# A two-layer attention trunk on one core: layer 0's SiLU gate in wide products, rope's swap in one operation, more gating from PSUM, and a new order

## The chip, the core and the metric

The kernel runs on one core of a Trainium2 chip. The metric is device microseconds for one execution, the median over runs. Five engines matter: TensorE (PE) multiplies, with its weight loads shown apart (PEld); VectorE (DVE) and ScalarE (ACT) do the elementwise work; GpSimd (POOL) does a few powers; the Sync engine (SP) issues the loads. Each engine takes its instructions in the order in which they are written and waits at semaphores.

## The reference

256 tokens of width 1024 pass two layers. Both normalise, project to queries, keys, values and a gate `z`, mix the tokens, multiply by `silu(z)`, project out and add; then each adds a projected embedding under a sigmoid gate.

```python
for i in range(DEPTH):                       # DEPTH = 2
    h = rms_norm(x, norm_gain[i])
    x = x + (moba_layer if i % 2 == 0 else nsa_layer)(h, ...)
    gate = jax.nn.sigmoid(rms_norm(x, ple_gate_gain[i]) @ ple_w_gate[i])
    x = x + gate * (p[i] @ ple_w_proj[i])

def moba_layer(h, w_in, q_gain, k_gain, w_out, pos):      # layer 0
    q, k, v, z = jnp.split(h @ w_in, 4, axis=-1)
    q = rope(rms_norm(split_heads(q, N_HEADS), q_gain), pos)
    k = rope(rms_norm(split_heads(k, N_HEADS), k_gain), pos)
    o = merge_heads(moba_attention(q, k, v)) * jax.nn.silu(z)
    return o @ w_out

def rope(x, pos):                                          # halves of a head change places
    x1, x2 = xf[..., :half], xf[..., half:]
    return jnp.concatenate([x1 * cos - x2 * sin, x2 * cos + x1 * sin], axis=-1)
```

With 256 tokens and blocks of 256, layer 0 is causal attention over 16 heads of 64. Layer 1 has 16 query heads in 4 groups, and three branches per head (compressed keys, selected blocks, window), each weighted by a sigmoid and summed.

## The kernel before

Precision: a weight matrix arrives in float32 and is split into a high part (`hi`, rounded, written by ACT) and a low part (`lo`, the remainder, written by DVE). Activations are split the same way into a tile `a` that holds high and low side by side, 256 columns each. A product is `hi`x`a`-high + `hi`x`a`-low + `lo`x`a`-high.

Two classes hold the projections with features on the partitions. `Unit` takes 512 output features; for each slice of 128 of the contraction and each block of 128 features, `mul` issues three products of 256 columns into one half of a PSUM bank. `Wide` takes 256 features; it multiplies `hi` by both halves of `a` in one product of 512 columns, a whole bank, and adds `lo` x high as a product of 256 into the bank's left half. What leaves a `Wide` bank has to be joined: right half plus left half. The list `WIDE` names the projections done so: before, the output projections and embedding gates of both layers (`o0 o1 g0 g1`, and with `n` those of layer 1); `z0 z1`, layer 0's gate, are `Unit`s.

`tail` is the part of a layer from `z` on. A gate that comes from a `Unit` leaves through `evac_z` (512 columns, two blocks: scale by the token's norm, tanh, one product), one from a `Wide` through `evac_wz`, which no step before the change uses. Attention output for two blocks (a group, 0 to 3) stands in one bank of tag `tr`. Step `E<g>` copies it to `oT` by ACT, and `x.<k>` multiplies a block by its gate and splits it into `a`; step `G<g>` (`gate_o`) multiplies the bank by the gate in one DVE operation, and `x.<k>` then only splits. Before, every group goes through `E`.

In layer 1 the compressed branch of a group is added in one of two ways: step `<g>B` makes its transposed weights `pcT` and `pcL` ahead, and the group's `V` step then adds its four products to its own bank; or step `<g>b`, later, multiplies into a bank of its own, and DVE adds that to `oT`. Before, group 3 has a `B` and groups 0, 1 and 2 have a `b`.

`rope` works on 8 heads and two blocks of 128 tokens. Per block, `turn` multiplies the swapped halves by the sine table: `turn(t, 0)` and `turn(t, 1)`, 256 columns each. Seven ropes run: four in layer 0 (`q`, `k`, `1q`, `1k`), three in layer 1 (`KE`, `QE0`, `QE1`).

The order: `PROGRAM` is a list of some 500 steps, written out by hand. A step records operations, and a planner (`Plan.schedule`) with a cost per operation then sets each engine's order among all that is ready, earlier-recorded first; it may also move an operation made with `nc.copy` from ACT to DVE. In the list, `w:name.i` loads and splits a weight tile, `name.i` multiplies it, `name>b` empties a bank; `A S T V` are a head pair's transposes, scores, transposed weights and products with the values. Buffers limit what can run ahead: five of each of `raw`, `hi`, `lo` and `tmp`, four PSUM banks `mm`, two `tr`, two `s`.

Of the kernel before, what the change touches and what calls it, by code (L numbers as in the profile page):

```python
# [19 lines left out]
SWITCH, POW = 150.0, 2300.0  # L20
NRAW, NHI, NLO, NPT, NA = 5, 5, 5, 9, 9
WARM = 14
WIDE, NARROW = "o0 o1 g0 g1 no0 no1 ng0 ng1", "ng1b"
MARGIN = 100.0

PROGRAM = ("x0 w:c0 c0 x1 w:c1 c1 x2 w:c2 x3 w:c3 x4 w:c4 w:k.0 x5 c2 w:c5 c3 x7 consts tq a.1 x6 a.3 a.5 a.6 w:c6 a.7 w:c7 "
# [24 lines left out]

STORES = 5

# [8 lines left out]
class View:  # L62
# [25 lines left out]
    def box(self):  # L88
        (ps, pn), free = self.ap.ap[0], self.ap.ap[1:]
        p0, f0 = divmod(self.ap.offset, ps)  # L90
        return p0, p0 + pn, f0, f0 + sum((n - 1) * s for s, n in free) + 1

    def elems(self):
        n = 1
# [326 lines left out]
def trunk(ctx: ExitStack, tc: tile.TileContext, a, out):  # L421
# [14 lines left out]
    def tmp(name):  # L436
        return work.tile([P, 512], F32, tag="tmp", name=name, bufs=5)
# [136 lines left out]
    class Wide:  # L574
# [2 lines left out]


        def __init__(self, src, xs, wide=True):
            self.src, self.xs, self.w, self.ps, self.wide = src, xs, {}, None, wide  # L580

        def weights(self, g):
            if self.ps is None:
# [85 lines left out]
    def rope(ps, tab, nb, norm, is_q, tag, bufs, o=None):  # L669
        if o is None:  # L670
            o = work.tile([P, 2, 512], F32, tag=tag, name=tag, bufs=bufs)
        else:
            ps = [o[:, t] for t in range(2)]
        o = o.rearrange("p t (h d) -> p t h d", d=HD)
        ssq = work.tile([P, 2, 8], F32, tag="ssq", name="ssq")
        for t in range(2):
            sq = tmp("hsq").rearrange("p (h d) -> p h d", d=HD)
            nc.scalar.activation(sq.rearrange("p h d -> p (h d)"), ps[t], AF.Square)
            nc.vector.tensor_reduce(ssq[:, t], sq, axis=AX.X, op=OP.add)
        r0 = work.tile([P, 2, 8], F32, tag="r0", name="r0")  # L680
        g = 8 // nb
        qss = [tmp("qs").rearrange("p (b g d) -> p b g d", b=nb, d=HD) for _ in range(2)]
        vs = [ps[t].rearrange("p (b g d) -> p b g d", b=nb, d=HD) for t in range(2)]

        def tb(i, t, lo, hi):
            return tab[:, i, t, :, None, lo:hi].to_broadcast([P, nb, g, hi - lo])

        def turn(t, c):
            lo, hi = 32 * c, 32 * c + 32
            nc.vector.tensor_tensor(qss[t][:, :, :, lo:hi], vs[t][:, :, :, 32 - lo:64 - lo], tb(1, t, lo, hi), op=OP.mult)  # L690

        since = len(nc.ops)
        for t in range(2):
            nc.vector.tensor_scalar(r0[:, t], ssq[:, t], 1.0 if is_q else 1.0 / HD,
                                    norm.e2[:, 0 if is_q else 1, t:t + 1], op0=OP.mult, op1=OP.add)

        turn(0, 0)
        nc.together(since)
        r = work.tile([P, 2, 8], F32, tag="r_" + tag, name="r_" + tag, bufs=bufs)
        nc.gpsimd.tensor_tensor(r.rearrange("p t h -> p (t h)"), r0.rearrange("p t h -> p (t h)"), neg_half, op=OP.pow)  # L700
        if is_q:
            nr = work.tile([P, 2, 8], F32, tag="nr_" + tag, name="nr_" + tag, bufs=bufs)
            nc.vector.tensor_scalar(nr, r, -1.0, None, op0=OP.mult)
        def finish():
            for t in range(2):
                ot = o[:, t].rearrange("p (b g) d -> p b g d", b=nb)
                if t:
                    turn(t, 0)
                turn(t, 1)
                nc.vector.tensor_tensor(ot, vs[t], tb(0, t, 0, HD), op=OP.mult)  # L710
                nc.vector.tensor_tensor(ot, ot, qss[t], op=OP.add)
                if not is_q:
                    nc.vector.tensor_tensor(o[:, t], o[:, t], r[:, t, :, None].to_broadcast([P, 8, HD]), op=OP.mult)

        return o, (nr if is_q else None), finish
# [13 lines left out]
    def flat(ap):  # L729
        return ap.rearrange("p a b -> p (a b)")  # L730
# [6 lines left out]
        nc.scalar.activation(th, zr, AF.Tanh, scale=0.5)  # L737
        nc.vector.scalar_tensor_tensor(flat(zz[:, m:m + 2]), flat(th), 1.0, flat(zr), op0=OP.add, op1=OP.mult)

    def evac_wz(zz, ps, m, norm):  # L740
        zr, th = tmp("zr")[:, :T], tmp("th")[:, :T]
        nc.scalar.activation(zr, ps[:, T:], AF.Copy)
        nc.vector.tensor_tensor(zr, zr, ps[:, :T], op=OP.add)
        nc.vector.tensor_tensor(zr, zr, norm.bc, op=OP.mult)
        nc.scalar.activation(th, zr, AF.Tanh, scale=0.5)
        nc.vector.scalar_tensor_tensor(zz[:, m], th, 1.0, zr, op0=OP.add, op1=OP.mult)

    def tail(i, oT, pvs, zin, xz, norm, after):

# [52 lines left out]
        def wide(kind, h, xs, evac):  # L802
            name = f"{n}{kind}{h}"
            if name not in WIDE.split():
                return False
            for q in range(2):
                u = Wide(a["w_" + name][q], xs, name + "ab"[q] not in NARROW.split()).steps(name + "ab"[q])
                for b in range(2):
                    todo[f"{name}{'ab'[q]}>{b}"] = lambda u=u, b=b, m=4 * h + 2 * q + b: evac(u, b, m)
            return True  # L810
# [23 lines left out]
                    after(k)  # L834

        for h in range(2):
            if not wide("z", h, xz, lambda u, b, m: evac_wz(zz, u.ps[b], m, norm)):
                u = Unit(zin[h], True, xz).steps(f"{n}z{h}")
                for b in range(2):
                    todo[f"{n}z{h}>{b}"] = lambda u=u, b=b, m=4 * h + 2 * b: evac_z(zz, u, b, m, norm)  # L840
# [698 lines left out]
```

## Time and profile before

| | |
|---|---|
| Median of 3 runs | 358.29 us (358.08 to 359.67) |
| Profiled execution | 359.04 us, span 357.2 us |
| Granted TensorE clock | 1.000 |
| Instructions in the span | 6734 |
| Read from memory | 57.46 MB, 164 GB/s over the span |
| Queues | 20160 of 20770 packets in SP's queue |

The profile's page gives busy time per engine, the chain of work that ended last, and groups of instructions (engine, operation, out<-in, shape, count, then busy us and the mean ns of one, then the idle time before them and what ended it). Nearly all operations carry the line of the planner's emitting loop (L399), so groups are told apart by tile names and shapes: `mm<-a,hi` is a projection's product, `tr<-cst,sm` a transpose of attention weights, `big` holds `oT`, gates and the like, `tq` and `tk` are rope's tables. Matmuls are pipelined, and the mean of one is longer than the distance from one to the next; distances are read from start times.

### The profile page before, as it was taken

Reading aid. Unit: us, or ns where it says so; the run is one execution under the profiler, and the core shown is the slowest. Engines: PE = TensorE matmul, PEld = TensorE weight load, DVE = VectorE, ACT = ScalarE, POOL = GpSimd, SP = SyncE. Lnnn points to the kernel's source line nnn. Section 1 sums busy time; section 2 is a strip of 40 time slices with the busy share of each in tenths; the row PEclk is TensorE's granted clock in tenths of the full one; section 3 lists DMA queues with packets and bytes.
Section 4 is the critical chain, followed back from the end, with each engine's and each line's share of the span. In section 5 each row is a group of like instructions: output and inputs, shape, how many; then the busy total and the mean of one; then the engine's idle time right before and its main releaser. Section 6 shows DMA issues by size and latency. Waiting matters only on the chain.

```text
span 357.2 us, 6734 instructions
## 1 busy us (share of the span) xinstructions
PE 351.3 (98%) x2327; PEld 308.4 (86%) x2327; DVE 334.0 (93%) x845; ACT 276.6 (77%) x614; POOL 30.0 (8%) x26
## 2 busy tenths in 40 slices
PE   8999999999999999999999999999999999999995
PEld 6788888888999888888889999866998989888884
DVE  4899999999999988989989999999999999999985
ACT  4775699998999865758844988968979999947632
POOL 1033200320000000010003300003000000000100
PEclk9999999999999999999999999999999999999999
DMA  7988665053653455664453625347573432166012
GB/s 249 338 332 274 232 218 194 1 184 132 200 166 117 153 176 171 190 198 153 127 175 100 237 75 178 120 150 284 205 240 137 125 111 63 61 217 194 0 47 73
DMA packets 20770, 58.95 MB, mean 165 GB/s; under 512 B 2560, under 2 KB 6016, under 8 KB 20736
## 3 DMA queue, kind: packets, MB, share of 16 engines
q1 hardware_dynamic: 20160, 58.04, 50.0%
q10 hardware_dynamic: 576, 0.48, 0.4%
q8 instruction: 18, 0.29, 0.3%
q14 instruction: 16, 0.13, 0.1%
HBM read 57.46 MB, written 1.05 MB: 164 GB/s over the span
## 4 chain that ended last, share of the span: by engine, by line
PE 97%; DMA 1%; DVE 0%; ACTq 0%; issue 0%; ACT 0%; DVEq 0%
PE mm L399 77%; PE tr L399 13%; PE s L399 6%; DMA tmp<-in_wq 1%; ACTq L399 0%; DVE tmp L399 0%; DVE hi L399 0%; ACT tmp L399 0%; DVE xT L399 0%; DVEq L1534 0%
## 5 line engine op out<-in xcount | busy, mean ns | idle before, releaser
L399 PE MATMUL mm<-a,hi 128*128 128x256 f32 (+1 forms) x656 | 154.0, 327 | 0.0
L399 ACT ACTIVATE hi<-raw 128x1024 fp32r<-128x1024 f32 (+2 forms) x100 | 99.6, 1007 | 35.3 <-PE mm L399 20.9
L399 DVE TENSOR_TENSOR lo<-raw,hi 128x1024 fp32r<-128x1024 f32 (+2 forms) x100 | 115.1, 1161 | 6.3 <-ACT hi L399 5.8
L399 PE MATMUL mm<-a,lo 128*128 128x256 f32 x448 | 104.6, 283 | 0.0
L399 PE MATMUL mm<-hi,a 128*128 128x512 f32 (+2 forms) x356 | 102.1, 377 | 0.5 <-DVE hi L399 0.5
L399 PEld LDWEIGHTS mm<-a,hi 128*128 128x128 f32 x656 | 101.2, 190 | 0.8 <-issue 0.2
L399 PEld LDWEIGHTS mm<-a,lo 128*128 128x128 f32 x448 | 83.2, 189 | 10.1
L399 PEld LDWEIGHTS mm<-hi,a 128*128 128x128 f32 x356 | 64.5, 191 | 11.9 <-ACT a L399 0.6
L399 PE MATMUL mm<-lo,a 128*128 128x512 f32 (+2 forms) x178 | 63.6, 374 | 0.0
L399 ACT ACTIVATE sm<-sm,nb 128x128 f32<-128x128 f32 (+1 forms) x96 | 42.6, 448 | 3.8 <-DVE nb L399 3.6
L399 PEld LDWEIGHTS mm<-lo,a 128*128 128x128 f32 x178 | 33.0, 188 | 5.4 <-DVE lo L399 0.2
L399 DVE CUSTOM_DVE_ANT_0 sm<-s,cst,nr_q 128x128 f32<-128x128 f32 (+1 forms) x96 | 35.8, 410 | 0.4
L399 ACT ACTIVATE tmp<-tmp 128x256 f32<-128x256 f32 (+3 forms) x26 | 12.2, 472 | 13.3 <-DVE tmp L399 13.0
L399 ACT ACTIVATE pt<-tr 128x384 f32<-128x384 f32 x48 | 21.7, 483 | 0.6 <-PE tr L399 0.3
L399 PE MATMUL tr<-cst,sm 128*128 128x128 f32 x144 | 22.0, 275 | 0.0
L399 POOL TENSOR_TENSOR r_q<-r,neg_half 128x16 f32<-128x16 f32 x5 | 14.6, 2925 | 76.9 <-DVE r L399 76.9
L399 PEld LDWEIGHTS tr<-cst,sm 128*128 128x128 f32 x144 | 16.8, 141 | 3.2 <-ACT sm L399 0.8
L399 POOL TENSOR_TENSOR rstd<-ms,neg_half 128x2 f32<-128x2 f32 x4 | 4.7, 1184 | 165.9 <-DVE ms L399 165.9
L399 ACT ACTIVATION_READ_ACCUMULATOR sm<-sm,nb 128x1 f32 x96 | 18.3, 191 | 0.0
L399 ACT ACTIVATE a<-xT,gain_in 128x256 fp32r<-128x256 f32 x31 | 14.5, 498 | 4.7 <-DMA xT<-in_x 1.9
L399 DVE TENSOR_TENSOR hl<-tr,hl 64x512 fp32r<-64x512 f32 x24 | 16.5, 689 | 1.7 <-ACT hl L399 1.1
L399 DVE TENSOR_SCALAR sm<-sm,l 128x128 f32<-128x128 f32 (+1 forms) x67 | 17.8, 315 | 0.1
(167 smaller groups left out, 453.1 us busy)
## 6 DMA issues: line engine op xcount, KB each, us to landing
raw<-in_moba_in SPq DMA_DIRECT2D x28, 512.0 KB, 4.5
raw<-in_nsa_in SPq DMA_DIRECT2D x24, 512.0 KB, 4.0
raw<-in_w_o SPq DMA_DIRECT2D x8, 512.0 KB, 3.9
raw<-in_w_g SPq DMA_DIRECT2D x8, 512.0 KB, 3.8
raw<-in_w SPq DMA_DIRECT2D x8, 512.0 KB, 3.7
raw<-in_w_no SPq DMA_DIRECT2D x8, 512.0 KB, 4.3
raw<-in_w_ng SPq DMA_DIRECT2D x8, 512.0 KB, 3.8
raw<-in_ple_proj SPq DMA_DIRECT2D x4, 512.0 KB, 4.1
```

Of the source, the lines that this page charges most:

```text
L399: getattr(getattr(self.nc, o.engine), o.method)(*[real(x) for x in o.args], **{k: real(x) for k, x in o.kwargs.items()})
```

## The change

Layer 0's gate is put on the list `WIDE`, so that its products are made by `Wide`, and `evac_wz` is rewritten to join two banks into one tile of 512 columns before it scales it. Rope's `turn` becomes one operation over both halves, with a reversed step over the axis of the halves (`View.box`, which finds what an operation touches, learns negative steps). The list uses `G2`, `G3` and `nG3` in the place of `E2`, `E3` and `nE3`, and `2B` in the place of `2b`. The list is written in another order from `masks` on; its last steps are as before.

```diff
-WIDE, NARROW = "o0 o1 g0 g1 no0 no1 ng0 ng1", "ng1b"
+WIDE, NARROW = "o0 o1 g0 g1 no0 no1 ng0 ng1 z0 z1", "ng1b"
...
-           "w:1q.0 w:1q.3 1q.0 masks w:1k.0 A2 S2 w:1k.2 w:1q.1 w:1q.2 A3 1k.0 1k.1 w:1v.0 S3 1q.1 1q.2 1q.3 1qe A0 1q T2 "
+           "w:1q.0 w:1q.3 1q.0 masks w:1k.0 v A3 S3 w:1q.1 1q.1 w:1q.2 1q.2 1q.3 w:1k.3 A2 w:1v.0 w:1v.1 A0 1qe S2 1q T3 "
...
-        def turn(t, c):
-            lo, hi = 32 * c, 32 * c + 32
-            nc.vector.tensor_tensor(qss[t][:, :, :, lo:hi], vs[t][:, :, :, 32 - lo:64 - lo], tb(1, t, lo, hi), op=OP.mult)
+        def turn(t):
+            v, q = (x.rearrange("p b g (c d) -> p (b g) c d", c=2) for x in (vs[t], qss[t]))
+            nc.vector.tensor_tensor(q, v[:, :, ::-1], tb(1, t, 0, HD).rearrange("p b g (c d) -> p b g c d", c=2), op=OP.mult)
...
-        turn(0, 0)
+        turn(0)
...
                 if t:
-                    turn(t, 0)
-                turn(t, 1)
+                    turn(t)
...
-    def evac_wz(zz, ps, m, norm):
-        zr, th = tmp("zr")[:, :T], tmp("th")[:, :T]
-        nc.scalar.activation(zr, ps[:, T:], AF.Copy)
-        nc.vector.tensor_tensor(zr, zr, ps[:, :T], op=OP.add)
-        nc.vector.tensor_tensor(zr, zr, norm.bc, op=OP.mult)
+    def join(u, m):
+        b, first = m % 2, u.sum is None
+        if first:
+            u.sum = tmp("sum")
+        half = u.sum[:, b * T:b * T + T]
+        nc.scalar.activation(half, u.ps[b][:, T:], AF.Copy)
+        nc.vector.tensor_tensor(half, half, u.ps[b][:, :T], op=OP.add)
+        return not first
+
+    def evac_wz(zz, u, m, norm):
+        if not join(u, m):
+            return
+        zr, th, m = u.sum, tmp("th"), m - m % 2
+        zr2 = zr.rearrange("p (a b) -> p a b", a=2)
+        nc.vector.tensor_tensor(zr2, zr2, norm.bc[:, None, :].to_broadcast([P, 2, T]), op=OP.mult)
         nc.scalar.activation(th, zr, AF.Tanh, scale=0.5)
-        nc.vector.scalar_tensor_tensor(zz[:, m], th, 1.0, zr, op0=OP.add, op1=OP.mult)
+        nc.vector.scalar_tensor_tensor(flat(zz[:, m:m + 2]), flat(th), 1.0, flat(zr), op0=OP.add, op1=OP.mult)
```

What this does to the engines' order is shown at three places. First TensorE, in layer 0's gate, before: `hi` and `lo` are the weight's parts (here the ones loaded, since features lie on the partitions), `a` the moving activations, `mm_78` and `mm_79` the two banks.

```order
L399 MATMUL mm_78<-a_112,hi_117 128x256 x2
L399 MATMUL mm_78<-a_112,lo_122 128x256
L399 MATMUL mm_78<-a_112,hi_117 128x256 x2
L399 MATMUL mm_78<-a_112,lo_122 128x256
L399 MATMUL mm_79<-a_112,hi_117 128x256 x2
L399 MATMUL mm_79<-a_112,lo_122 128x256
```

The same engine in the changed kernel's gate:

```order
L401 MATMUL mm_78<-a_107,hi_114 128x512
L401 MATMUL mm_78<-a_108,hi_114 128x512
L401 MATMUL mm_78<-a_107,lo_119 128x256
L401 MATMUL mm_78<-a_108,lo_119 128x256
L401 MATMUL mm_79<-a_105,hi_114 128x512
L401 MATMUL mm_79<-a_106,hi_114 128x512
```

Two slices now share a bank's stretch, with one product of 512 and one of 256 each. In all, 192 products of 256 columns become 64 of 512 and 64 of 256.

Second VectorE, at the end of layer 0's gate and the start of the gated output, before: `tmp<-mm,bc` scales two blocks from PSUM, `big_89` is the gate, `big_88` is `oT`.

```order
L399 TENSOR_TENSOR tmp_84<-mm_80,bc_137 128x512
L399 TENSOR_TENSOR lo_121<-raw_124,hi_116 128x1024
L399 SCALAR_TENSOR_TENSOR big_89<-tmp_85,tmp_84 128x512
L399 TENSOR_TENSOR tq_0_129<-cst_65,gnsa_67 128x128 x2
L399 SCALAR_TENSOR_TENSOR big_88<-big_89,big_88 128x256 x4
L399 TENSOR_TENSOR a_110<-big_88,a_110 128x256
```

The same place in the changed kernel, with `tmp<-tmp,mm` the join of a bank's halves, and `big_88<-big_89,tr` a group gated from its bank:

```order
L401 SCALAR_TENSOR_TENSOR big_89<-tmp_82,tmp_84 128x512
L401 TENSOR_TENSOR tmp_83<-tmp_83,mm_79 128x256
L401 SCALAR_TENSOR_TENSOR big_88<-big_89,tr_75 128x512
L401 TENSOR_TENSOR tmp_83<-tmp_83,bc_137 128x512
L401 TENSOR_TENSOR lo_121<-raw_127,hi_117 128x1024
L401 SCALAR_TENSOR_TENSOR big_89<-tmp_85,tmp_83 128x512
L401 TENSOR_TENSOR a_110<-big_88,a_110 128x256
L401 SCALAR_TENSOR_TENSOR big_88<-big_89,tr_76 128x512
```

Four block products on SBUF are gone, one per group from PSUM stands there, and the joins stand among them.

Third TensorE, at the end of group 2's products with the values in layer 1, before: `pt` are the transposed weights, `pcT` and `pcL` the compressed branch's.

```order
L399 MATMUL tr_75<-pcT_187,vcB_101 128x256
L399 MATMUL tr_75<-pcL_99,vcB_101 128x256
L399 MATMUL tr_75<-pcT_187,vcB_101 128x256
L399 MATMUL tr_75<-pcL_99,vcB_101 128x256
L399 MATMUL tr_76<-cst_65,sm_71 128x128 x3
L399 MATMUL mm_78<-a_110,lo_122 128x256
```

The changed kernel at `2V`:

```order
L401 MATMUL tr_75<-pt_166,v_96 64x256
L401 MATMUL tr_75<-pt_162,v_96 64x256
L401 MATMUL tr_75<-pt_166,v_96 64x128
L401 MATMUL tr_75<-pt_162,v_96 64x128
L401 MATMUL tr_75<-pcT_187,vcB_101 128x256
L401 MATMUL tr_75<-pcL_99,vcB_101 128x256
L401 MATMUL tr_75<-pcT_187,vcB_101 128x256
L401 MATMUL tr_75<-pcL_99,vcB_101 128x256
L401 MATMUL tr_76<-cst_65,sm_68 128x128 x3
```

The four products of the compressed branch of group 2, which stood by themselves after group 2's bank had been emptied, now follow directly on the products with the values, into the same bank.

More of the change, by code (lines that the diff above doesn't have):

```diff
@@ L90, in box @@
         p0, f0 = divmod(self.ap.offset, ps)
-        return p0, p0 + pn, f0, f0 + sum((n - 1) * s for s, n in free) + 1
+        ends = [(n - 1) * s for s, n in free]
+        return p0, p0 + pn, f0 + sum(min(e, 0) for e in ends), f0 + sum(max(e, 0) for e in ends) + 1
     def elems(self):
@@ L579, in __init__ @@
         def __init__(self, src, xs, wide=True):
-            self.src, self.xs, self.w, self.ps, self.wide = src, xs, {}, None, wide
+            self.src, self.xs, self.w, self.ps, self.wide, self.sum = src, xs, {}, None, wide, None
         def weights(self, g):
@@ L738, in evac_z @@
         nc.vector.scalar_tensor_tensor(flat(zz[:, m:m + 2]), flat(th), 1.0, flat(zr), op0=OP.add, op1=OP.mult)
-    def evac_wz(zz, ps, m, norm):
-        zr, th = tmp("zr")[:, :T], tmp("th")[:, :T]
-        nc.scalar.activation(zr, ps[:, T:], AF.Copy)
-        nc.vector.tensor_tensor(zr, zr, ps[:, :T], op=OP.add)
-        nc.vector.tensor_tensor(zr, zr, norm.bc, op=OP.mult)
+    def join(u, m):
[12 more added lines that the diff above has]
+        nc.vector.tensor_tensor(zr2, zr2, norm.bc[:, None, :].to_broadcast([P, 2, T]), op=OP.mult)
         nc.scalar.activation(th, zr, AF.Tanh, scale=0.5)
-        nc.vector.scalar_tensor_tensor(zz[:, m], th, 1.0, zr, op0=OP.add, op1=OP.mult)
+        nc.vector.scalar_tensor_tensor(flat(zz[:, m:m + 2]), th, 1.0, zr, op0=OP.add, op1=OP.mult)
     def tail(i, oT, pvs, zin, xz, norm, after):
@@ L836, in tail @@
         for h in range(2):
-            if not wide("z", h, xz, lambda u, b, m: evac_wz(zz, u.ps[b], m, norm)):
+            if not wide("z", h, xz, lambda u, b, m: evac_wz(zz, u, m, norm)):
                 u = Unit(zin[h], True, xz).steps(f"{n}z{h}")
```

45 rows, old and new, of the table PROGRAM are left out of this document.

## The prediction

> **What bounds the kernel now.** The first view is the page's table of busy time, then the chain that ended last by engine.
>
> ```profile
> PE 351.3 (98%) x2327; PEld 308.4 (86%) x2327; DVE 334.0 (93%) x845; ACT 276.6 (77%) x614; POOL 30.0 (8%) x26
> PE 97%; DMA 1%; DVE 0%; ACTq 0%; issue 0%; ACT 0%; DVEq 0%
> ```
>
> A busy PE alone proves little, since its ends are modelled, but the chain also lies on it for 97% of the span. The view of waits, asked for PE's matmuls, says what it waits for:
>
> ```profile
> PE tr L399 <- DVE ones L399: 1.1, 1, 1.1
> PE mm L399 <- DVE hi L399: 0.5, 1, 0.5
> ```
>
> Two waits in the whole program. The chain in order of time puts both into the head, and shows what remains behind the last product:
>
> ```profile
> 1.65 4.78 DMA tmp<-in_wq
> 6.45 0.44 DVE hi L399
> ...
> 7.03 12.64 PE mm L399 x53
> ...
> 338.86 14.13 PE mm L399 x96
> 353.01 0.30 DVE tmp L399
> ```
>
> So the time is a head of 7.0 us, 346 us (7.03 to 353.0) in which TensorE takes one product after another, and a tail of 4.2 us to 357.2. What the change takes from PE's stream it takes from the time; what it does on the other engines counts only where PE comes to wait for it. VectorE is the one that could make it wait:
>
> ```profile
> 20.00:125.00 105.00, 105.00 (x690) 92.90 (x689) 102.90 (x239) 90.80 (x191) 15.14 (x7) 1.00 0.54 179
> 125.00:200.00 75.00, 75.00 (x422) 65.62 (x423) 69.81 (x143) 49.02 (x86) 5.63 (x4) 1.00 0.54 163
> 200.00:313.00 113.00, 112.85 (x890) 99.90 (x889) 110.60 (x353) 102.23 (x275) 6.65 (x6) 1.00 0.45 151
> ```
>
> The columns are stretch, length, PE, PEld, DVE, ACT, POOL, clock, DMA share. DVE has 2.1 us free in layer 0's attention (20 to 125), 5.2 in its projections (125 to 200), 2.4 in layer 1's attention. The granted clock is 1.00 throughout, and DMA stands near half.
>
> **The gate's products (PE).** Layer 0's `z` has 64 tiles (8 slices of the contraction by 8 column blocks). Each takes three products of 256 columns now, and one of 512 and one of 256 then: 192 products become 128, over the same 768 columns a tile. The price of a narrow tile is in the chain's pieces that hold nothing but them; that of a wide tile in the timeline of layer 0's gate projection, where each row is the start of two 512-column products, with two 256-column ones behind it.
>
> ```profile
> 98.84 5.75 PE mm L399 x48
> ...
> 106.16 5.76 PE mm L399 x48
> ```
>
> ```profile
> 142.19 0.63 PE L399 MATMUL mm<-a,hi 128*128 128x512 f32 x2
> ...
> 146.37 0.63 PE L399 MATMUL mm<-a,hi 128*128 128x512 f32 x2
> ```
>
> Narrow: 5.75/48 = 0.1198 a product, 0.3594 a tile. Wide: the two rows are six rounds of two tiles apart, (146.37 - 142.19)/12 = 0.3483. The difference, 0.0111, by 64 tiles is **-0.71 us**, all of it on the bounding engine. It is small because PE's pace goes by columns and the columns stay.
>
> That is also where a rule can be weighed. The Trainium skill (TensorE: Matmul & The Clock Gate, Back-to-back issue gap) gives a sustained spacing of about 81 ns for 128 columns and 131 ns for 512, so that a wide product costs far less per column. An estimate from that page puts 256 columns at some 98 ns, a tile at 229 instead of 294 ns, and the change at -4.2 us. The rows above do not agree: two 512s and two 256s take 0.697 us, which leaves 0.229 for a 512.
>
> **The rest of the change (DVE and ACT).** No product, transpose or score matmul is added or dropped elsewhere. The prices come from the groups kept apart by shape:
>
> ```profile
> L399 DVE TENSOR_TENSOR tmp<-mm,tq 128x256 f32<-128x256 f32 x12 | 4.9, 418 | 0.0
> L399 DVE TENSOR_TENSOR q<-q,tmp 128x512 f32<-128x512 f32 x10 | 6.7, 685 | 0.0
> L399 DVE TENSOR_TENSOR tmp<-tmp,mm 128x256 f32<-128x256 f32 x14 | 5.8, 416 | 0.4 <-ACT tmp L399 0.4
> L399 ACT ACTIVATE tmp<-mm 128x256 f32<-128x256 f32 x14 | 5.2, 369 | 1.7 <-PE mm L399 1.7
> L399 DVE SCALAR_TENSOR_TENSOR big<-big,big 128x256 f32<-128x256 f32 x16 | 6.4, 421 | 0.2
> L399 DVE SCALAR_TENSOR_TENSOR big<-tmp,tmp 128x512 f32<-128x512 f32 x8 | 5.5, 691 | 0.4 <-ACT tmp L399 0.4
> L399 ACT ACTIVATE big<-tr 128x512 f32<-128x512 f32 x8 | 4.7, 594 | 1.8 <-PE tr L399 1.4
> L399 DVE TENSOR_TENSOR big<-big,tr 128x512 f32<-128x512 f32 x3 | 2.0, 683 | 0.0
> L399 DVE TENSOR_TENSOR big<-big,pe 128x480 f32<-128x480 f32 x4 | 3.8, 985 | 0.0
> ```
>
> - `evac_wz`: each of 8 banks now needs its halves joined, a copy on ACT and an add on DVE: 8 x 0.416 = +3.33 on DVE, 8 x 0.369 = +2.95 on ACT. The scaling, tanh and last product stay four of 512 columns.
> - Rope: 28 swaps of half a head (0.418) become 14 of 512 columns. The trace has no operation with a reversed axis. Below, it costs what any two-source one of that size does, 0.685; above, the nearest strided row, the windows at 985 ns for 480 elements, scales to 1.05. I take 0.685, since the halves swapped now (0.418) cost as much as unswapped operations of their size (0.416): 11.70 to 9.59, -2.11 (-1.21 in layer 0's four ropes, -0.90 in layer 1's three).
> - Three groups gated from PSUM: per group, an evacuation on ACT (0.594) and two DVE products (0.842) become one DVE product of 512 (0.691, the row of its shape): -0.45 on DVE, -1.78 on ACT.
> - Group 2's branches summed in PSUM: one DVE add less, -0.68. Its four products now close the bank's sum in `2V` instead of filling a bank of their own.
>
> DVE: 3.33 - 2.11 - 0.45 - 0.68 = +0.09; ACT: +1.17. But the place changes. Layer 0 gains 3.33 - 1.21 - 0.30 = +1.82 on DVE and layer 1 loses 0.90 + 0.15 + 0.68 = 1.73. In 20 to 125 DVE would then want 102.9 + 1.8 = 104.7 of the 104.3 that PE leaves. I cost this at nothing: the 0.4 too much can run into the next stretch, whose 5.2 us of free DVE are its cover. If the new order needed it all at once, it would be +0.4. In layer 1 the free 2.4 us become some 4.
>
> **Moves and waits.** The program's list is unchanged up to `masks w:1k.0` and in its last steps, so head and tail stay. Of what is moved, the loads are the same 140 DMAs; eight of `moba_in` become eight of `w_z` of equal size, and a load lands in about 4 us:
>
> ```profile
> raw<-in_moba_in SPq DMA_DIRECT2D x28, 512.0 KB, 4.5
> raw<-in_w_o SPq DMA_DIRECT2D x8, 512.0 KB, 3.9
> ```
>
> PSUM banks of `z` and of the half-done `1v` are now held across each other's steps, and the pair's sum holds a temporary until its second half is there; what queues behind such a hold is ACT's and DVE's work, and PE only if that runs out of lead. `2V` now waits for `2B`'s copies; behind it in PE's queue stand the transposes of group 3 and `nz1`'s products, so a late copy would stop PE for it. Today's largest wait for such a copy is a weight load's 0.4, behind running products:
>
> ```profile
> PEld tr L399 <- ACT pt L399: 1.1, 3, 0.4
> ```
>
> Bounds for the order as a whole: up, a few such waits, 0 to +2; down, what PE's stream wastes now. That is seen in groups of equal make:
>
> ```profile
> 116.39 0.65 PE tr L399 x6
> ...
> 238.88 0.81 PE tr L399 x6
> ...
> 244.87 0.81 PE tr L399 x6
> ...
> 247.55 0.81 PE tr L399 x6
> ...
> 254.32 0.13 issue
> ```
>
> Six transposes cost 0.65 in layer 0 and 0.16 more at three places of layer 1; with the issue gap that is 0.6 us, and I allow twice that, 1.2, for what pieces of mixed make hide. I take 0 for the order: PE has no wait to lose, and DVE's work is the same in sum.
>
> **The sum.** The profiled execution took 359.04 (span 357.2, 1.8 around it). With -0.71 for `z` and 0 for the rest it becomes 358.3; it lies 0.75 above the median of 358.29, which becomes **357.6**. Half a per cent, 1.8 us, is about what can be told from no change; 0.71 is less.
>
> **Rivals.**
> - *The order also recovers PE's waste.* For it: the 0.16s above, all in layer 1, where everything is reshuffled. Against: under 1 us of it shows. At the full 1.2: 357.6 - 1.2 = 356.4, with spread down to 355.7. Chance 0.22.
> - *New small waits eat the gain* (`2V` behind `2B`, a held bank): two to four of 0.4 give 358.4 to 359.2. For it: a stream without waits can only gain some. Chance 0.10, counted as no change.
> - *VectorE becomes the bound in layer 0*, the case on the other side. Place: 20 to 125, where DVE would be 100% full; what makes it decide is the reversed swap. Eight of the 14 lie there. At 1.05 each instead of 0.685 the overrun is 0.4 + 8 x 0.365 = 3.3 us, and the time 357.6 + 3.3 = 360.9; layer 1's six (+2.2) fit into its 4 free. It is slower by more than 1.8 from an overrun of 2.5, a swap of 0.95. For it: DVE's 2.1 us. Against: today's half swaps cost nothing extra. The Trainium skill (Vector Engine (DVE) Microarchitecture Reference, Performance modes) lists a negative step among what was not measured, and no run here shows it yet. Chance 0.15, which takes in any other way to such an overrun.
> - *Weight loads, not columns, set the pace.* Then a tile of two loads takes 2 x 0.1198, and the time falls by 64 x 0.1198 = 7.7 to 349.9. This is how the rule on spacing would show here. The wide rows speak against it: two loads take 0.348 there. Chance 0.03.
>
> The forecast itself has 0.50, with 357.0 to 358.3 as its own range. Faster by over 0.5%: 0.22 + 0.03 = 0.25; within: 0.50 + 0.10 = 0.60; slower: 0.15. The range reaches from 355.6 (the recovered waste) to 360.6 (the overrun with a swap just short of 1.05); outside stay the loads' case, half of the overrun's, and the tails, some 0.15.
>
> **What would show it.** Right: 64 fewer PE products and pieces of wide `z` at 0.348 a tile; a reversed swap near 0.685; DVE about 334 us, with more before and less after 200; PE still without waits after 7 us. Wrong: waits of PE or its weight loads for DVE between 20 and 125, or for ACT's `pcT` copy before `2V`; a swap over 0.95; six transposes of layer 1 at 0.65 throughout, or a span that shrinks by more than z's term.

## The result and the profile after: slower by half a per cent

The changed kernel took 360.53 us in the median of 7 runs (360.01 to 361.58), the kernel before 358.49 beside it: a ratio of 1.0053 with a 95% interval of 1.0036 to 1.0071. Forecast were 357.6 us and, as likeliest, no change that can be told; the time lies near the upper end of the range (355.6 to 360.6), on the slower side. The profiled execution took 360.77 us.

The page's busy time and the chain by engine, of the changed kernel:

```profile
PE 351.7 (98%) x2263; PEld 304.8 (85%) x2263; DVE 335.4 (93%) x840; ACT 275.4 (77%) x614; POOL 31.8 (9%) x26
PE 87%; DVE 3%; ACT 3%; DMA 3%; POOL 1%; issue 1%; SPq 1%; ACTq 0%; DVEq 0%
```

The 64 products are gone, DVE's sum has hardly moved, and still the chain lies on PE for 87% instead of 97%; a part of that is a late load in the head, but POOL is on it too, which it was not before. The view of waits for PE's matmuls has five rows instead of two:

```profile
PE tr L401 <- DVE ones L401: 1.1, 1, 1.1
PE s L401 <- ACT qk L401: 0.6, 1, 0.6
PE mm L401 <- DVE hi L401: 0.4, 1, 0.4
PE mm L401 <- ACT hi L401: 0.3, 1, 0.3
PE mm L401 <- DVE tmp L401: 0.2, 1, 0.2
```

The prices that the forecast rested on came out (groups by shape, changed kernel: the reversed swap, and the joins with others of their shape):

```profile
L401 DVE TENSOR_TENSOR tmp<-mm,tq 128x512 f32<-128x512 f32 x6 | 4.1, 684 | 0.0
L401 DVE TENSOR_TENSOR tmp<-tmp,mm 128x256 f32<-128x256 f32 x22 | 9.0, 411 | 0.3 <-ACT tmp L401 0.2
```

So did the wide tile's: in TensorE's timeline, these two rows of two 512-column products, with two of 256 behind each, are three rounds of two tiles apart: 2.09/6 = 0.348 a tile, as forecast (0.3483).

```profile
100.84 0.62 PE L401 MATMUL mm<-a,hi 128*128 128x512 f32 x2
...
102.93 0.63 PE L401 MATMUL mm<-a,hi 128*128 128x512 f32 x2
```

And VectorE did not fill up (windows of the stretch that held 105.00, 102.90 of DVE before):

```profile
20.00:125.00 105.00, 104.06 (x618) 88.23 (x619) 101.18 (x237) 89.99 (x194) 17.12 (x7) 1.00 0.51 166
```

It idled 3.8 of 105 us there, and PE fell short by 0.9. A part of the idling is a wait of its own, shown below; but also in e9, further down, where TensorE is busy for all of this stretch, VectorE has 102.97, against 102.90 before. What is dear is not how much DVE does, but when.

**Where the time is.** Each norm brings its sums of squares together on TensorE (`tr<-ones,sqacc`). Between norm `a`, ahead of layer 0's attention, and norm `b`, the next, both kernels push exactly the same 272,648 columns through TensorE, and behind `b` the same 413,324, so these marks cut the work alike. TensorE's timeline, first before and then after (start, duration; the last row is the last product):

```profile
19.51 0.51 PE L399 MATMUL tr<-ones,sqacc 128*128 128x2 f32 x4
150.08 0.50 PE L399 MATMUL tr<-ones,sqacc 128*128 128x2 f32 x4
352.58 0.40 PE L399 MATMUL mm<-a,lo 128*128 128x256 f32 x2
```

```profile
19.59 0.51 PE L401 MATMUL tr<-ones,sqacc 128*128 128x2 f32 x4
151.44 0.50 PE L401 MATMUL tr<-ones,sqacc 128*128 128x2 f32 x4
354.31 0.40 PE L401 MATMUL mm<-a,lo 128*128 128x256 f32 x2
```

From `a` to `b`: 130.57 before, 131.85 after, +1.28, although the gate should have taken 0.71 off. Behind `b`: 202.50 and 202.87, +0.37. Together +1.65; the medians stand 2.04 apart.

**The late power.** The chain of the changed kernel in order of time leads from TensorE to POOL and back over two engines:

```profile
62.53 0.36 DVE r L401 x2
62.96 5.03 POOL r_q L401
68.35 0.58 issue
68.93 0.69 DVE hl L401
69.65 1.22 DVE lo L401
```

`r_q` is the inverse square root for the rope of `1q`, 16 elements raised to a power. POOL's timeline has it before (first) and after:

```profile
63.53 3.01 POOL L399 TENSOR_TENSOR r_q<-r,neg_half 128x16 f32<-128x16 f32 x1 [25.16 <-DVE r L399]
```

```profile
62.96 5.01 POOL L401 TENSOR_TENSOR r_q<-r,neg_half 128x16 f32<-128x16 f32 x1 [24.92 <-DVE r L401]
```

The same instruction takes 2.00 us more. VectorE's timeline beside it, changed kernel:

```profile
62.79 0.68 DVE L401 TENSOR_TENSOR tmp<-q,tq 128x512 f32<-128x512 f32 x1
63.40 1.21 DVE L401 TENSOR_TENSOR lo<-raw,hi 128x1024 fp32r<-128x1024 f32 x1
64.53 0.68 DVE L401 TENSOR_TENSOR q<-q,tq 128x512 f32<-128x512 f32 x1
65.13 0.17 DVE L401 RECIPROCAL l<-l 128x4 f32<-128x4 f32 x1
...
65.80 0.68 DVE L401 TENSOR_TENSOR q<-q,tmp 128x512 f32<-128x512 f32 x1
68.01 0.17 DVE L401 TENSOR_SCALAR nr_q<-r_q 128x16 f32<-128x16 f32 x1 [1.53 <-POOL r_q L401]
68.21 1.41 DVE L401 TENSOR_TENSOR hl<-tr,hl 64x512 fp32r<-64x512 f32 x2
```

From 62.79 on VectorE runs three operations without a break that read two tensors from SBUF each (swap, weight remainder, product with the cosine), until a small one with one source starts at 65.13. The power ends at 67.97, 2.84 after that, and where the swaps read from PSUM the trace has it at 2.90 (POOL, layer 1):

```profile
189.76 2.90 POOL L401 TENSOR_TENSOR r_q<-r,neg_half 128x16 f32<-128x16 f32 x1 [2.26 <-DVE r L401]
```

So the power seems to have begun only where that run of operations ended. Once it has begun, such operations do not seem to stretch it: the first rope's power in the changed kernel, at 23.80, starts beside a swap that reads from PSUM, two weight remainders run during it, and it takes 2.90. The trace of before has the same in small, at the power of two elements that each norm takes (POOL, then VectorE at the second of them):

```profile
186.92 0.70 POOL L399 TENSOR_TENSOR rstd<-ms,neg_half 128x2 f32<-128x2 f32 x1 [34.18 <-DVE ms L399]
```

```profile
151.03 1.72 POOL L399 TENSOR_TENSOR rstd<-ms,neg_half 128x2 f32<-128x2 f32 x1 [70.28 <-DVE ms L399]
```

```profile
150.96 1.22 DVE L399 TENSOR_TENSOR lo<-raw,hi 128x1024 fp32r<-128x1024 f32 x1
```

At 186.92 VectorE reduces a single tensor. At 151.03 a weight remainder has just begun, VectorE's next row (one source) starts at 152.10, and the power ends 0.65 after that.

Back to the changed kernel: `nr_q` stands where a power of ordinary length would have been ready; it is an instruction in VectorE's queue, so VectorE stood 1.53 us, with `hl` behind it, ScalarE's `qk` behind that, and TensorE's scores (`s`) behind `qk`. The kernel before has the same step, with the swap in four pieces and no weight remainder in it; its reader on VectorE came 0.6 us after the power's end at 66.54:

```profile
67.14 0.17 DVE L399 TENSOR_SCALAR nr_q<-r_q 128x16 f32<-128x16 f32 x1
```

The Trainium skill (SBUF — State Buffer, Who interferes with whom) says that a VectorE instruction with two SBUF inputs contends with a GpSimd instruction that reads SBUF. The 5.01 us agree with it; that the power waits out three such instructions in a row is in the trace alone. The prediction did not weigh it.

### The profile page after: what moved, and what is told of

Read it like the earlier page. It is cut to its first block, busy times and chain, and to the rows that moved or that the text cites. A ratio compares the mean times of both kernels' runs of the same rounds, so it can differ in the third digit from the quotient of the medians.

```text
span 359.0 us, 6585 instructions
## 1 busy us (share of the span) xinstructions
PE 351.7 (98%) x2263; PEld 304.8 (85%) x2263; DVE 335.4 (93%) x840; ACT 275.4 (77%) x614; POOL 31.8 (9%) x26
## 4 chain that ended last, share of the span: by engine, by line
PE 87%; DVE 3%; ACT 3%; DMA 3%; POOL 1%; issue 1%; SPq 1%; ACTq 0%; DVEq 0%
PE mm L401 69%; PE tr L401 12%; PE s L401 5%; DMA xT<-in_x 2%; POOL r_q L401 1%; DMA tmp<-in_wq 1%; ACT hi L401 1%; DVE sm L401 1%; DVE lo L401 1%; SPq L401 1%; ACT sm L401 1%; ACT tmp L401 0%; DVE hl L401 0%; DVE q L401 0%; DVE tmp L401 0%
## 5 line engine op out<-in xcount | busy, mean ns | idle before, releaser
L401 PE MATMUL mm<-a,hi 128*128 128x512 f32 (+1 forms) x592 | 150.5, 344 | 0.2 <-DVE tmp L401 0.2
L401 PE MATMUL mm<-a,lo 128*128 128x256 f32 x448 | 98.0, 282 | 0.0
L401 PEld LDWEIGHTS mm<-a,hi 128*128 128x128 f32 x592 | 92.2, 190 | 1.9 <-DVE tmp L401 0.5
L401 PEld LDWEIGHTS mm<-a,lo 128*128 128x128 f32 x448 | 81.9, 189 | 12.1 <-issue 0.2
L401 PE MATMUL tr<-cst,sm 128*128 128x128 f32 x144 | 23.4, 276 | 0.1
L401 POOL TENSOR_TENSOR r_q<-r,neg_half 128x16 f32<-128x16 f32 x5 | 16.6, 3324 | 76.3 <-DVE r L401 76.3
L401 ACT ACTIVATE tmp<-mm 128x256 f32<-128x256 f32 (+2 forms) x34 | 14.5, 436 | 7.2 <-PE mm L401 6.9
L401 DVE TENSOR_SCALAR sm<-sm,l 128x128 f32<-128x128 f32 (+1 forms) x73 | 19.4, 314 | 0.1
```

The lines of the kernel that those rows point to most:

```text
L401: getattr(getattr(self.nc, o.engine), o.method)(*[real(x) for x in o.args], **{k: real(x) for k, x in o.kwargs.items()})
```

## The experiments

All are changes of the kernel after, unless said otherwise. Times are medians, ratios are to the kernel before run beside them (358.4 to 358.6).

**e1: the power's reader six rows later.** `nr_q` of `1q`'s rope on VectorE moves behind six of its followers; nothing else moves.

```diff
 TENSOR_TENSOR q<-q,tmp 128x512
-TENSOR_SCALAR nr_q<-r_q 128x16
 TENSOR_TENSOR hl<-tr,hl 64x512 x2
 TENSOR_TENSOR lo<-raw,hi 128x1024
 ...
+TENSOR_SCALAR nr_q<-r_q 128x16
```

> The changed kernel with a single instruction moved: VectorE's small product that turns GpSimd's power of rope 1q into -r (nr_q) stands six rows later in VectorE's order, behind two hl rows, two lo rows and two q rows; all other rows of all engines as in the changed kernel. Theory 1 (a wait in the order): in the profile after, VectorE stood 1.5 us at that product for a power that took 5.0 us, and PE lost 0.8 + 0.3 us at 70 to 73 us behind it; moved, these go and the time falls by 1.0 to 1.5 us, to 359.0 to 359.5. Theory 2 (load: VectorE has too much to do in layer 0, whatever the order): VectorE makes up nothing, the same time is lost later between 75 and 125 us, and the time stays within 0.3 us of 360.5.

Measured 359.09, ratio 1.0006 (0.9996 to 1.0017): 1.44 us below the changed kernel. From `a` to `b` it takes 130.42 instead of 131.85. The power still takes 5.01; nothing waits for it now. The largest single cause is shown. One wait of PE remains in the gate, the last of the five above (`tmp`, 0.2), and TensorE starts its next product there 0.59 us after the one before instead of 0.23. The rows on VectorE:

```profile
102.06 1.23 DVE L401 TENSOR_TENSOR lo<-raw,hi 128x1024 fp32r<-128x1024 f32 x1
103.31 0.42 DVE L401 TENSOR_TENSOR tmp<-tmp,mm 128x256 f32<-128x256 f32 x1
```

A join (`tmp<-tmp,mm`) that frees a bank stands behind a weight remainder of 1.23 us.

**e6: the remainder behind the second swap.** Here `lo<-raw,hi` of 63.40 moves behind the second swap, and `nr_q` stays. That remainder is then computed from its buffer's next load, and the products with it are not the reference's.

```diff
 TENSOR_TENSOR tmp<-q,tq 128x512
-TENSOR_TENSOR lo<-raw,hi 128x1024
 TENSOR_TENSOR q<-q,tq 128x512
 RECIPROCAL l<-l 128x4
 TENSOR_TENSOR tmp<-q,tq 128x512
+TENSOR_TENSOR lo<-raw,hi 128x1024
```

> The changed kernel with one VectorE row moved, another than in e1: the 1.2 us remainder lo<-raw,hi that stands between rope 1q's first and second reversed swap goes behind the second swap; the product that waits for GpSimd's power (nr_q) stays in its place. Theory 1a (GpSimd's power takes 5.0 us because VectorE runs long operations on SBUF while the power starts): the power falls from 5.0 to about 3.3 us, the value that e2b shows where two swaps follow each other, VectorE's wait of 1.5 us goes, and the time is that of e1, 358.9 to 359.4. Rival 1b (the power's length has to do with something else): 5.0 us stays, VectorE waits as before, 360.3 to 360.8.

The power fell to 3.28, and VectorE's wait for it is gone; POOL's and PE's rows:

```profile
62.02 3.28 POOL L401 TENSOR_TENSOR r_q<-r,neg_half 128x16 f32<-128x16 f32 x1 [24.64 <-DVE r L401]
```

```profile
PE mm L401 <- DVE lo L401: 1.4, 1, 1.4
```

So the remainder between swap and product is what stretches the power, by 1.73. The time did not follow: 360.35, ratio 1.0052 (1.004 to 1.0064), because the moved row now waited for its load and TensorE for the row. As a cure it is useless, as a reading of the power it is clear.

**e7: the reversed swap undone.** Each of the 14 swaps is issued as two halves, at its place in the new order.

```diff
-nc.vector.tensor_tensor(q, v[:, :, ::-1], ...)
+for lo in (0, 32):
+    nc.vector.tensor_tensor(qss[t][..., lo:lo + 32], vs[t][..., 32 - lo:64 - lo], ...)
```

> The changed kernel with each of its 14 reversed swaps issued as the two half swaps of before, back to back in the same place; no other row of any engine differs. It undoes the merge of rope's swap alone. By the price of the rows VectorE gets 14 x (2 x 0.418 - 0.685) = 2.1 us more work. Theory 1 (waits decide, VectorE's sum does not): 360.5 +- 0.5, and if the reversed step is what stretches the power of 1q, then that falls to about 3.0 us and the time to about 359.3. Theory 2 (VectorE's load in layer 0 decides): +1 to +2, 361.5 to 362.5.

361.02, ratio 1.0083 (1.0059 to 1.0107), with the power at 5.08. Not better, so the reversed step is not the cause. The time is at the upper edge of theory 1's; by the marks, `a` to `b` takes 132.06, 0.2 more than in the changed kernel.

**e3: the wide gate alone, in the old order.** The kernel before with the gate's new products and joins, its list kept.

```diff
-WIDE = "o0 o1 g0 g1 no0 no1 ng0 ng1"
+WIDE = "o0 o1 g0 g1 no0 no1 ng0 ng1 z0 z1"
```

> The kernel before with layer 0's gate in wide products alone, each old step replaced in its place by the two steps that do the same weights, the list otherwise that of before; the planner sets the engines' orders anew. If the term of the prediction holds and the joins are hidden: 357.5 to 358.0 (-0.7). Theory 2 (the joins' 3.3 us on VectorE are not hidden in layer 0): 359.5 to 361, with PE waiting for VectorE's joins or for what stands behind them between 85 and 125 us.

367.57, ratio 1.0239 (1.0214 to 1.0264), the slowest of all. PE's waits:

```profile
PE mm L400 <- DVE tmp L400: 1.5, 2, 0.8
PE s L400 <- ACT qk L400: 1.5, 2, 0.8
PE s L400 <- DVE nb L400: 1.2, 1, 1.2
PE s L400 <- DVE hl L400: 0.8, 1, 0.8
```

The wide gate alone costs 9 us in the old list, with the engines' orders set anew by the planner. These waits, six between 104 and 126 us, make 5.0 of it; the rest was not followed. In this order the joins are not hidden, so gate and order cannot be costed apart by it. Whether only the new list can hide them is not shown.

**e2 and e2b: one layer's order each.** e2 keeps the new list through layer 0 into its last projections and goes on with the old one, e2b the other way round (with the narrow gate and the old gating of its groups).

```diff
-PROGRAM = <the new list>
+PROGRAM = <new list to g0a.00> + <what is left of the old one>      # e2
+PROGRAM = <old list to w:g0a.1> + <what is left of the new one>     # e2b
```

> The changed kernel's code and its order up to the first products of layer 0's embedding gate; from there on the order of before (with its nE3 and 2b). Theory 1 and 2 both put the loss into layer 0: 359.8 to 360.8, as the changed kernel. Rival (the loss is spread over layer 1's new order and 2B): 358.5 or less.

> The other half: layer 0 in the order of before with its narrow gate products and its evacuations of groups 2 and 3, rope's swap in one operation, and layer 1 in the changed order with 2B and nG3. Theories 1 and 2: no loss left, 358.0 to 358.8. Rival (layer 1's new order costs): 359.3 or more.

e2: 362.71, ratio 1.0115 (1.0089 to 1.0142), 2 us over what either theory gave. From `a` to `b` it takes 131.84, as the changed kernel, with the power at 5.01; behind `b` it takes 205.33, 2.8 more than before although the list there is the old one; the planner set the engines' orders anew, and where the 2.8 us lie was not followed. So it tells little of layer 1. e2b: 359.73, ratio 1.0032 (1.002 to 1.0044), 0.8 below the changed kernel, with the power at 3.27. But from `a` to `b` it takes 131.64, 1.07 more than before: it has a wait of its own at 118 us (0.5, PE for VectorE), at which it falls back by 0.77. So a short power alone does not save layer 0, and this pair does not price the power; e1 does.

**e9: the join one row earlier too.** e1, and the third join stands ahead of the remainder.

```diff
+TENSOR_TENSOR tmp<-tmp,mm 128x256
 TENSOR_TENSOR lo<-raw,hi 128x1024
-TENSOR_TENSOR tmp<-tmp,mm 128x256
```

> e1 with one more VectorE row moved: the join of the gate's third bank, at 105 us, one row earlier, ahead of a 1.2 us remainder. In e1's profile PE waits 0.5 us there for this join, which frees the bank. Theory 1: the wait goes, -0.3 to -0.5 against e1, 358.6 to 358.8. Theory 2 (VectorE is full, so what is late there is then late elsewhere): no change against e1, 359.1.

> The same program as e9_join_earlier, so that the next two are compared with it on one chip. Both theories: 358.7, within 0.3 of the first measurement.

358.68, ratio 1.0005 (0.9993 to 1.0017), and in the second measurement 358.79, ratio 1.001 (0.9998 to 1.0022). In the first profile PE waits for nothing but its first operand. TensorE's marks:

```profile
18.85 0.51 PE L401 MATMUL tr<-ones,sqacc 128*128 128x2 f32 x4
148.89 0.50 PE L401 MATMUL tr<-ones,sqacc 128*128 128x2 f32 x4
351.79 0.40 PE L401 MATMUL mm<-a,lo 128*128 128x256 f32 x2
```

From `a` to `b` 130.04 (130.06 in the second), 0.38 under e1. In the run times the join is worth 0.3 to 0.4 by the medians and nothing by the ratios (1.0006 in e1): the traces tell it, the clock does not.

**e8 and e10: the gate's rate.** e1 and e9, with each of the gate's 64 wide products issued as two of 256 columns at its place (the expectation of e10 speaks of 32).

```diff
-nc.tensor.matmul(o, wh[:, j, s], both, start=k == 0, ...)
+nc.tensor.matmul(o[:, :T], wh[:, j, s], xh, start=k == 0, ...)
+nc.tensor.matmul(o[:, T:], wh[:, j, s], xl, start=False, ...)
```

> e1 (the changed kernel with nr_q later) with each 512-column product of layer 0's gate issued as two of 256 into the two halves of the bank; the joins and all other rows as in e1. It undoes the wide product alone. The prediction's term: 64 x (2 x 0.1198 - 0.229) = +0.7 us, so 359.8 if it is fully on the path. Rival (part of the gate stage waits for VectorE anyway, so a shorter product only lengthens a wait): +0.0 to +0.4.

> As e9_join_earlier (both waits gone), with each of the 32 512-column products of layer 0's gate issued as two of 256 at its place. Theory 1 (the wide products are worth their 0.71 us as soon as no wait stands behind them; in e8 the join's wait had hidden it): slower than e9_again by 0.5 to 0.8, about 359.4. Rival (TensorE's pace in the gate does not set the time even now, the products' results are waited for in any case): equal to e9_again within 0.2.

e8: 359.03, ratio 1.001 (1.0001 to 1.002), as e1, as its rival had it: while the join is late, TensorE's faster rate only lengthens its wait. In the traces e8 falls 0.31 behind e1 up to the join at 104 us, and makes up 0.29 there. e10: 358.66, ratio 1.0007 (0.9997 to 1.0017), as e9 by the clock. By the marks it takes 130.46 from `a` to `b`, 0.41 more than e9's two profiles. The 0.41 builds up in even small steps over the gate's products, from 86 to 107 us. So the rate is worth about 0.4 of its 0.71 there. It does not show in the time; the stretch behind `b`, which differs by 0.40 between e9's two profiles, may be why.

**b0: the kernel before, profiled again.**

> The kernel before, unchanged, for a second profile of it. Theory 1 (the profile of before that the prediction was summed on was a long run of that kernel, by a load that landed late in the head): about 358.4, with the 0.74 us step among the first products near 6 us gone or smaller, and the stretch from 20 to 313 us as long as in the first profile. Rival (the stretch itself was long in that profile, so the sum started from a wrong base): the stretch from 20 to 313 us is shorter here by about 0.6 us.

358.12. Its marks:

```profile
18.62 0.51 PE L399 MATMUL tr<-ones,sqacc 128*128 128x2 f32 x4
149.20 0.50 PE L399 MATMUL tr<-ones,sqacc 128*128 128x2 f32 x4
351.67 0.40 PE L399 MATMUL mm<-a,lo 128*128 128x256 f32 x2
```

130.58 and 202.47, within 0.03 of the first profile; the 0.9 us between the two executions lie in the head, where products wait for the first loads. So stretches between marks can agree to some hundredths where whole profiled times do not. They do not always: behind `b`, e9's two profiles are 202.90 and 203.30, and e15, below, takes 130.42 from `a` to `b` with e9's layer 0, as TensorE falls back by 0.4 us at 20 to 23 us.

**e11, e12, e13: small waits behind `b`.** e9 needs 202.90 and 203.30 from `b` to its last product, before 202.5. In e9, three places where TensorE stood 0.27, 0.25 and 0.15 us for a score's maximum were turned on VectorE. The kernel before stands at one of them too, for the same kind of row (`s<-v_1r,hl`, at 254.45), so that one is no part of the difference.

```diff
+ISA sm,nb<-s,cst,nr_q x2            # 212 us (e11, e12)
 TENSOR_TENSOR lo<-raw,hi 128x1024
-ISA sm,nb<-s,cst,nr_q x2
 ...
+ISA sm,nb<-s,cst,nr_q x2            # 252 us (e11, e12, e13); at 267 us likewise, with two vcB rows
 TENSOR_TENSOR tmp<-tmp 128x248
-ISA sm,nb<-s,cst,nr_q x2
```

> As e9_join_earlier, with three more turns of VectorE's order in layer 1, where TensorE stood still 0.27, 0.25 and 0.15 us for a score's maximum: at 212 us the weight remainder behind two score rows, at 252 us two small rows of the compression behind two score rows, at 267 us two value rows behind two score rows. Theory 1 (what is left in the layers is such small waits, each worth its own length): 0.4 to 0.7 below e9_again, about 358.1, a little below before. Rival (each cure makes the row that was moved back the next one late, as with the remainder in e6): equal to e9_again within 0.2.

> As e9_join_earlier, with the three turns of VectorE's order in layer 1 at 212, 252 and 267 us, the other engines' orders unchanged and every row reading what it read before. Theory 1 (layer 1 gives its time away in these waits, 0.27, 0.25 and 0.15 us, each worth its length): layer 1's stretch shorter by 0.4 to 0.7, time about 358.2. Rival (the remainder moved at 212 us is itself wanted at once, and TensorE waits for it instead): as e9, 358.7.

> As e9_join_earlier, with only the turns at 252 and 267 us (waits of 0.25 and 0.15 us), which move no weight remainder. Theory 1: 0.3 to 0.4 below e9, about 358.4, and above e12 by 0.3. Rival (the waits in layer 1 are slack that the next transfer takes back): as e9, 358.7.

e11 took 364.64 (ratio 1.018, 1.0165 to 1.0195), but there the moved remainder read its buffer's next load and waited for it, as in e6; it answers nothing. e12, with every row's inputs kept: 359.46, ratio 1.0023 (1.0013 to 1.0034). The wait that the rival named is there, behind the first turn: the remainder behind two score rows is the next one late. The time is 0.7 above e9, which neither gave.

```profile
PE mm L401 <- DVE lo L401: 0.7, 1, 0.7
```

e13, without that turn: 358.88, ratio 1.0011 (1.0002 to 1.0021), as e9. The waits at 252 and 267 us are gone from its trace, but TensorE stood for a key at 204 us, and the cause is a load (e13, PE's waits; then ScalarE's timeline in e9 and in e13):

```profile
PE tr L401 <- DVE k_1r L401: 0.4, 1, 0.4
```

```profile
197.32 0.63 ACT L401 ACTIVATE hi<-raw 128x512 fp32r<-128x512 f32 x1
```

```profile
198.38 0.63 ACT L401 ACTIVATE hi<-raw 128x512 fp32r<-128x512 f32 x1 [1.01 <-DMA raw<-in_nsa_vw]
```

The load landed a microsecond later in one execution, and ScalarE's queue carries that to the keys behind the conversion. Theory 1 for these turns is not shown.

**e14, e15, e16: that conversion out of the keys' way.** Its `hi` on ScalarE and its `lo` on VectorE move behind the four rows of keys; e15 adds e13's turns, e16 also splits the gate's products.

```diff
-ACTIVATE hi<-raw 128x512
 ACTIVATE v<-mm,rstd
 ACTIVATE k_0r<-tr x2
 ACTIVATE k_1r<-tr x2
+ACTIVATE hi<-raw 128x512            # lo<-raw,hi likewise on VectorE
```

> As e9_join_earlier, with the conversion of one value weight in layer 1 (its hi on ScalarE, its lo on VectorE, both 128x512) taken behind the four rows of keys that stood behind it; its products come 8 us after the load's first landing, so nothing waits for it. Theory 1 (layer 1's new order puts the conversion of a load that can be late ahead of keys that TensorE wants at 204 us): the wait at 204 us is gone in every run, 0.2 to 0.4 below e9 (358.7), about 358.4. Rival (the wait there is slack that the scores at 213 us take back): as e9.

> As e14, with the two turns of e13 (waits of 0.25 and 0.15 us at 252 and 267 us). Theory 1 (each small wait is worth its length): 0.3 below e14, about 358.1, 0.1% below before. Rival (slack): as e14.

> As e15, with the gate's wide products issued as two of 256 columns each. Theory 1 (the rate is worth 0.71 us where nothing waits; the traces of e9 and e10 show 0.41 of it in layer 0): 0.4 to 0.7 above e15. Rival (the gate's rate does not set the time): as e15 within 0.2.

All missed: 363.12, 362.69 and 364.99, ratios 1.0124 (1.0099 to 1.0149), 1.0106 (1.0079 to 1.0134) and 1.0188 (1.0161 to 1.0214). PE's waits in e14, and the loads on SP's queue (start, time from the first issue to the last), first in e9 and then in e14:

```profile
PE mm L401 <- ACT hi L401: 1.8, 1, 1.8
PE mm L401 <- DVE lo L401: 1.5, 1, 1.5
```

```profile
194.02 5.02 SPq L401 DMA_DIRECT2D raw<-in_nsa_in  x3
```

```profile
194.29 9.97 SPq L401 DMA_DIRECT2D raw<-in_nsa_in  x3
```

The moved remainder ends 5 us later, and the third of these loads, which by its time takes the buffer that the remainder frees, is issued 5 us later with it. ScalarE converts that load at 207.38, and behind this in its queue stands the `hi` that TensorE waits for (at 212.0; in e9 it is at 207.6). The wait for `lo` is for the moved remainder itself: it ends at 203.9, and its products, which the expectation held to be far off, were next in TensorE's queue at 202.3. e16 stands 2.3 us over e15, far more than the gate's rate is worth at all, so the times of this pair say nothing on the rate; in the traces e16 falls some 0.4 behind e15 over the gate, as e10 behind e9.

No version here beats the kernel before; e1, e9 and e10 cannot be told from it, since their intervals hold 1.

## Why the prediction was wrong

- **"Moves and waits": "I take 0 for the order: PE has no wait to lose, and DVE's work is the same in sum." This step failed.** The order cost 1.44 us at `1q`'s power (e1) and about 0.4 at a join (e9, by the marks). The bound named beside it, "a few such waits, 0 to +2", held about what happened; I took the value 0 in it. Where the bounding engine never waits, a reordering of the others has little to gain and waits to lose. The prediction said so in a rival (new small waits, 358.4 to 359.2) and gave it 0.10; it looked for them at `2V` and at held banks, and the largest was a single one of 1.4 us at `1q`.
- **The missed instruction.** "Moves and waits" asks what a move does to PE, ACT, DVE and the loads, and leaves POOL out. The power of 16 elements was never priced, nor what stands beside it, although its reader sits in VectorE's queue. The trace of before had the numbers: 3.01 us, 0.6 us from its end to its reader, and a power of two elements that takes 0.70 or, beside a remainder, 1.72.
- **"VectorE becomes the bound in layer 0" fell in both its parts.** The swap cost 0.68, not 0.95 or more, and VectorE was not full (102.97 of 105 us in e9, where 104.7 were forecast). The time came near that rival's 360.9 by another mechanism, so that it lies within the range is luck.
- **"The rest of the change", DVE +0.09:** the page shows +1.4 (334.0 to 335.4), and ACT fell by 1.2 where +1.17 was forecast. The sum left out that the planner moves operations between the two: six more `sm<-sm,l` and two more `qk<-hl` stand on VectorE than before (+2.6 us by their groups), two `pcT` copies and one `big<-tmp` fewer (-1.2). It was not what decided.
- **"The gate's products", -0.71: the price of a tile was right, the effect smaller.** A wide tile takes 0.348 where wide tiles stand side by side, but undoing the wide products costs 0.41 (e10 against e9), and in e8 almost nothing, since the join's wait took it. With the two waits cured, `a` to `b` takes 130.05 instead of 130.57: -0.52, of which 0.41 is this rate; the other 0.1 was not followed.
- **Behind `b` the new order costs 0.2 to 0.8** (202.72 in e10, 202.90 and 203.30 in e9, against 202.5), where 0 was taken and the likeliest rival hoped for a gain. A load that lands at varying times is one cause that the traces show. The rest is open: of the changes meant to show it, e12, e14 and e15 made another row late, and e13's gained nothing that can be told.
- **Sum by the runs:** -0.5 (layer 0 with both waits cured) + 1.4 (power) + 0.4 (join) + 0.2 to 0.8 (behind `b`) = +1.5 to +2.1; measured +2.04. The last term is the spread of profiles and not a forecast, so the sum holds no better than to half a microsecond.
- **Of the other rivals**, "the order also recovers PE's waste" found none: in the changed kernel's chain six transposes still take 0.81 at 238.82 and 246.53. (The chain of before has a fourth such place, 0.84 at 249.06, which the 0.6 us leave out.) "Weight loads set the pace" is excluded by the 0.348 a tile; its 349.9 also takes off the 0.71 and the 7.7 together, though the 7.7 are counted from the narrow tile and hold the 0.71, so its own time would have been 350.6.

## What to carry to other kernels

Where the bounding engine has no waits, cost a reordering by its tightest hand-overs and not by each engine's sum: for each result of another engine, look how long before its reader it is ready, and what the change puts beside its maker. A reader in an in-order queue passes its wait to everything behind it, and a small operation on a slow engine is the easiest to forget. Compare orders between marks that hold the same work, since a head that depends on loads moves whole times by more than such a change does.

## What the runs showed of the hardware that was not expected

GpSimd's power of 16 elements is not a fixed price: 2.90 us beside swaps that read from PSUM, 3.01 with the old half swaps, 3.27 with the new swap in the old order, 5.01 with swap, remainder and product back to back on VectorE, 3.28 once the remainder is taken out. If it takes 2.90 once begun, it got in after the first swap in the last case, and in the changed kernel only after three operations; what decides at which boundary it gets in, no run here shows. The reversed step costs VectorE nothing (0.684 us against 0.685 for a forward operation of that size).
